# The last scan group of a Mamba-2 layer joins the common chunk order, and two products of the output projection take its place as filler

## The chip, the cores and the metric

The kernel runs on one core of one Trainium2 chip. The metric is the time of one execution on the device in microseconds (us). A core has five engines that run side by side, each with a queue of its own that it works through in order: TensorE (PE in the profile; its weight loads are PEld), VectorE (DVE), ScalarE (ACT), GpSimd (POOL) and SyncE (SP), which here does nothing but issue DMAs. ScalarE and GpSimd issue DMAs too. All transfers of the core share 16 DMA engines. An instruction waits on semaphores for what it reads and for the buffer that it writes, and everything behind it on its engine waits with it.

## The reference, cut to what matters

The program is two layers on 1024 tokens of width 1024 in float32, each with a residual: layer A is a chunked spatial gating MLP, layer B a Mamba-2 mixer, and a final RMSNorm follows. The change is in layer B:

```python
proj = h @ w_in                                   # 1024 x 6176: z | x | B | C | dt
xbc = silu(causal_depthwise_conv(xbc, conv_w, conv_b))        # 4 taps
# 8 groups g of 256 channels (4 heads), 8 chunks c of 128 tokens
cb = einsum('bclgn,bcsgn->bclsg', Cm, Bm)
w_ls = cb[..., None] * decay * dt[:, :, None]
y_diag = einsum('bclsgj,bcsgjp->bclgjp', w_ls, x)
states = einsum('bclgn,bclgj,bclgjp->bcgjpn', Bm, decay_to_end * dt, x)
# the state is carried from chunk to chunk: carry * dec + st
y_off = einsum('bclgn,bcgjpn,bclgj->bclgjp', Cm, prev, exp(dA_cs))
y = y_diag + y_off + x * d_skip
gated = rmsnorm_by_group(y * silu(z), norm_w)     # 8 groups of 256 channels
out = gated @ w_out                               # 2048 -> 1024, plus residual, then the final norm
```

## The kernel before, in words

**Products.** A float32 product is made of three products of rounded halves: an operand is split into a high part (a cast, by ScalarE, L111) and a low part (operand minus high part, by VectorE, L112), and `mm3` issues high·high, low·high and high·low (L134 to L136). "A step" below is six such matmuls of 128x128 by 512 columns. Large products are done as Strassen-Winograd schemes of seven products on half matrices (`Block` for the input projections, `Out` for the output projections); their sums of operand blocks are made on the way, for the input projection by VectorE and GpSimd (L204, L205 and neighbours), for the output projection by DMAs that add into SBUF (`add`, L682; `b12_plus`, L648 and L653; tiles ya and wb), which GpSimd issues.

**Layer B, input side.** `z_block(b)` makes the gate silu(z) of two groups as one Strassen block, and stores it to DRAM in `z_d`. Blocks 0 to 2 are 256 columns wide per half; block 3 is 128 wide, and makes the gate of group 6 alone. `Scan`'s other inputs x, B, C come from `xbc_block` for some groups, and for groups 2, 4, 6 and 7 from plain products by the generator `pj` (128 steps in all, tile ab). `convolve` puts the four convolution taps behind them on VectorE (L1182, and L1185 for the halo, tiles xc and bc).

**The scan.** `scans()` (written out by hand in `tc.manual_schedule()`) runs 56 chunks, groups 0 to 6 with 8 chunks each, in one pipeline. In chunk n it issues: `pe_b(n)` (four products on TensorE: L1427, L1431, L1437); steps of `pj` up to a target; `pe_a(n+2)` (transposes and C·B, L1395, L1396, tile tp); `update` and `out` (VectorE and GpSimd); `weights(n+1)` (L1419: the masked decay weights wl, which `pe_b(n+1)` needs); `decay(n+2)` (ScalarE, L1401, L1403; reads the tile wl that `load` fetched from cs_d, L1390); `tokens(n+2)` (L1409, L1411); `gate(n)` (L1470, GpSimd, by the gate tile ze); the queue of convolution taps, cleared by `drain`; `load(n+3)`. Half groups end with their sum of squares, a store of the gated result to DRAM (`g_d`, L1477), and, a group later, the inverse RMS (`rs_d`). `prefetch` brings a group's gate (L1359) and the decay broadcasts (L1362) into ze. The 128 steps of `pj` are spread over these 56 chunks, 16 ahead and 2 in each chunk, and so TensorE has 12 `mm3` matmuls beside the chunk's own 19 small ones.

**Group 7.** It comes behind `scans()`, and the tile scheduler orders it. `z_last` makes its gate as a plain product (96 matmuls of 512 columns) straight into SBUF (`Z`), so that group 7 needs neither `z_d` nor `g_d`. `last_steps` runs its 8 chunks with VectorE in the places where the other groups use GpSimd. `interleave` mixes these with `bo_first`: products 1 and 7 of the output projection `bo`, 32 steps, 192 matmuls (tile bo).

**The output projection.** `bo` is an `Out` with A = the gated result (tokens by 2048 channels) and B = the weight b_w_out. `fetch(n, c)` loads what product n needs of channel group c: A pieces ya (`load_a`, through `gscale`, which first loads the inverse RMS broadcast to 128 partitions, tile rb, L1649; then the piece, L1657; and then multiplies by norm weight and inverse RMS on VectorE, L1660) and B pieces wb (L642, 1 MB each). `prep(n, c)` splits both operands into xh, xl and wh, wl, and issues the sums by DMA. Products 2, 6, 4, 5 and 3 follow in `into_end`, where the residual is added (L792), the final norm is made and the result is stored.

Of the kernel before, what the change touches and what calls it, by code (L numbers as in the profile page):

```python
# [29 lines left out]
def kernel(  # L30
# [567 lines left out]
    class Out:  # L598
# [12 lines left out]
        def __init__(self, src, w, scale, res, accs, keep, ran):  # L611
# [3 lines left out]
            self.Y3 = []  # L615
# [9 lines left out]
        def load_a(self, i, kh, c):  # L625
# [30 lines left out]
        def prep(self, n, c):  # L656

            if (n, c) in self.ops:
# [4 lines left out]
                              6: ((0, 0), (0, 0)), 4: ((1, 1), (1, 0)), 5: ((1, 0), (0, 1))}[n]  # L663
            x, y = A(i, j, c), B(k, l, c)
# [5 lines left out]
            if n == 1:  # L670
                self.add(x, self.src[c][:, :, 512:1024] if self.scale is None else A(1, 0, c))
# [208 lines left out]
    def z_block(b, eng=nc.vector):  # L880

        wide = 256 if b < 3 else 128

        def done(name, i, a, u):
# [6 lines left out]
            g, m = (2 * b + j, i) if b < 3 else (6, j)  # L891
            nc.gpsimd.dma_start(out=z_d[g][:, m, th * 512:(th + 1) * 512], in_=zt)

        def W(kh, j):
            c = 512 * b + j * wide
            return [b_w_in[kh * 512:(kh + 1) * 512, c:c + wide]]

        return Block(H2, W, False, done, eng, wide)
# [32 lines left out]
    SPILT, AHEAD, LEFT = (0, 1, 3, 5), 16, 4  # L931
# [399 lines left out]
    def z_last(Z):  # L1331

        c = (G - 1) * 256
        W = [load_w([b_w_in[kh * 512:(kh + 1) * 512, c:c + 256]], 4) for kh in range(2)]
        for th in range(2):
            az = acc2("az")
            for kh in range(2):
                for m in range(2):
                    for k in range(4):
                        mm3(az[:, m, :], [w[:, k, m * P:(m + 1) * P] for w in W[kh]],  # L1340
                            [h_[:, k, :] for h_ in H2[f"A{2 - th}{kh + 1}"]], kh == 0 and k == 0, kh == 1 and k == 3)
                    if (kh, m) == (1, 1):
                        nc.scalar.activation(Z[:, :, th * 512:(th + 1) * 512], az, AF.Silu)
                    yield

# [5 lines left out]
    def prefetch(g, th):  # L1351
# [6 lines left out]
        if g < G - 1:  # L1358
            nc.sync.dma_start(out=ze[:, 0:2], in_=z_d[g][:, :, th * 512:(th + 1) * 512])  # L1359
# [6 lines left out]
    class Scan:  # L1366


        def __init__(self, g, eng):
            self.g, self.st, self.eng = g, sts[g], eng  # L1370
            self.wl, self.tp, self.cw, self.ps, self.state = {}, {}, {}, {}, {}
            if g < G - 1:
                gd.append(dr.tile([P, 2, T], F32, name=f"g_d{g}"))
            else:
                gd.append(self.st["Z"])
# [6 lines left out]
        def z(self, c, n=1):  # L1382
            if self.g == G - 1:
                return self.st["Z"][:, :, c * P:(c + n) * P]
            return self.st["ze", c // 4][:, 0:2, c % 4 * P:(c % 4 + n) * P]
# [87 lines left out]
        def squares(self, th):  # L1473
            sq = self.sq = q4([P, 2, 512], "gsq")
            nc.scalar.activation(sq, self.z(4 * th, 4), AF.Square)
            if self.g < G - 1:
                nc.sync.dma_start(out=gd[self.g][:, :, th * 512:(th + 1) * 512], in_=self.z(4 * th, 4))  # L1477
# [4 lines left out]
        def sum_b(self):  # L1482
            pr = sm("pr")
            n = 1 if self.g < G - 1 else 2
# [34 lines left out]
    def last_steps():  # L1519

        sc = Scan(G - 1, V)

        def a(c):
            sc.load(c), sc.pe_a(c), sc.decay(c), sc.tokens(c), sc.weights(c)

        a(0)
        yield
        for c in range(8):
            if c < 7:
                a(c + 1)  # L1530
                yield
            sc.pe_b(c), sc.carry(c), sc.update(c), sc.out(c)
            last = sc.gate(c)
            if c == 1:
                prefetch(G - 1, 1)
                rs = group_rstd(G - 2, 0, T)
            if c in (2, 3):
                rs[c - 2](last)
# [8 lines left out]
    def scans():  # L1547
# [33 lines left out]
        for n, (g, c) in enumerate(chunks):  # L1581
# [35 lines left out]
            if c == 4:  # L1617
                prefetch(g + 1, 0)
# [175 lines left out]
```

## Time and profile before

| | us |
|---|---|
| median of 3 runs | 1633.78 |
| lowest, highest run | 1629.82, 1635.27 |
| the profiled execution, own time | 1631.56 |
| its span in the trace | 1629.8 |
| chunk 53 of `scans()` to the end of products 1 and 7 (1377.14 to 1498.48) | 121.34 |
| products 2, 6, 4, 5, 3 with the end (1498.48 on) | 131.3 |

At 1377.14 the first matmul of chunk 53 of `scans()` (group 6, sixth chunk) starts. The span is the time from the first to the last recorded instruction. Busy times of engines are sums over the span; the share of a window has to be read for that window. The granted clock (PEclk) is the share of TensorE's full speed. A timeline row has the start in the span, the duration, engine, line, operation, tiles, and in brackets the idle time of the engine before it with the instruction or DMA that ended it. In the rows of the prediction "q1" is the DMA queue that SyncE feeds, and "q0" the one that GpSimd feeds.

### The profile page before, as it was taken

To read this page: it belongs to the slowest core of one execution; us is meant where nothing else is said; L and a number is where in the kernel's file an instruction comes from. 1 tells how busy PE (TensorE), PEld (TensorE's weight loads), DVE (VectorE), ACT (ScalarE), POOL (GpSimd) and SP (SyncE) were. 2 spreads that over 40 slices of the span, in tenths; PEclk is the share of its full clock that TensorE was granted. 3 is DMA by queue.
4 is the path that set the end of the run, shared out by engine and by line. 5 is a ranking of instruction groups with operands and counts; after the bars stand their busy time and mean duration, and the time that the engine had idled before them with its cause. 6 is when DMAs were issued, how large, how long until landed. Compare 5 with 4: busy or idle time off the path is not lost. (4 is left out here: it accounts for less than half of the span.)

```text
span 1629.8 us, 21273 instructions
## 1 busy us (share of the span) xinstructions
PE 1511.3 (93%) x7832; PEld 1245.5 (76%) x7832; DVE 1082.9 (66%) x1669; ACT 757.1 (46%) x1239; POOL 468.3 (29%) x477
## 2 busy tenths in 40 slices
PE   5799999999999897997899999999999999979988
PEld 5799988888888786775678777777777777757766
DVE  6966566666666543667744788587767767658656
ACT  4523233332324254544544454456667567544444
POOL 3601100000000231134203222407766756321231
PEclk8899999999999999998999999999999999989999
DMA  5154323333335999631253222447666575796993
GB/s 170 48 186 142 104 85 109 108 109 104 102 107 185 292 279 253 133 107 52 92 101 118 87 98 78 151 159 194 182 181 180 159 197 134 217 252 185 226 239 108
DMA packets 164872, 244.89 MB, mean 150 GB/s; under 512 B 16048, under 2 KB 96800, under 8 KB 161568
## 3 DMA queue, kind: packets, MB, share of 16 engines
q1 hardware_dynamic: 134672, 166.43, 34.6%
q0 software_dynamic: 20928, 63.45, 16.9%
q10 hardware_dynamic: 9168, 13.64, 2.3%
q8 instruction: 62, 1.02, 0.3%
q14 instruction: 42, 0.34, 0.1%
HBM read 169.23 MB, written 51.18 MB: 135 GB/s over the span
## 5 line engine op out<-in xcount | busy, mean ns | idle before, releaser
L134 PE MATMUL acc<-hh,wh 128*128 128x512 f32 x868 | 345.5, 398 | 14.5 <-ACT wh L111 4.0
L136 PE MATMUL acc<-hh,wl 128*128 128x512 f32 x868 | 343.4, 396 | 4.3 <-DVE wl L112 3.5
L135 PE MATMUL acc<-hl,wh 128*128 128x512 f32 x868 | 342.9, 395 | 4.4 <-DVE hl L964 4.4
L112 DVE TENSOR_TENSOR wl<-wr,wh 128x1024 fp32r<-128x1024 f32 x94 | 122.8, 1309 | 127.8 <-ACT wh L111 127.7
L134 PEld LDWEIGHTS acc<-hh,wh 128*128 128x128 f32 x868 | 166.2, 191 | 52.1 <-DVE u L1217 5.2
L136 PEld LDWEIGHTS acc<-hh,wl 128*128 128x128 f32 x868 | 165.8, 191 | 42.1 <-DVE wl L112 5.7
L135 PEld LDWEIGHTS acc<-hl,wh 128*128 128x128 f32 x868 | 166.1, 191 | 38.8 <-DVE hl L964 4.8
L111 ACT CAST wh<-wr 128x1024 fp32r<-128x1024 f32 (+1 forms) x113 | 116.2, 1030 | 113.7 <-PE acc L135 79.2
L252 ACT COPY u<-acc 128x512 f32<-128x512 f32 x117 | 68.0, 582 | 183.9 <-PE acc L136 182.6
L136 PE MATMUL acc<-wh,hl 128*128 128x256 f32 x448 | 130.8, 292 | 11.6 <-DVE hl L355 11.6
L134 PE MATMUL acc<-wh,hh 128*128 128x256 f32 x448 | 131.5, 293 | 4.1 <-DVE vt L291 2.5
L135 PE MATMUL acc<-wl,hh 128*128 128x256 f32 x448 | 130.1, 290 | 1.3 <-DVE wl L365 1.3
L1401 ACT ACTIVATE wl<-wl,tk 128x128 f32<-128x128 f32 x256 | 82.1, 392 | 86.3 <-DMA wl<-cs_d 85.9
L134 PE MATMUL ab<-hh,wh 128*128 128x512 f32 x256 | 116.5, 455 | 1.8 <-DVE u L1217 1.8
L112 DVE TENSOR_TENSOR xl<-ya,xh 128x1024 fp32r<-128x1024 f32 x40 | 48.9, 1223 | 80.1 <-ACT xh L111 79.9
L136 PE MATMUL ab<-hh,wl 128*128 128x512 f32 x256 | 101.3, 396 | 0.0
L135 PE MATMUL ab<-hl,wh 128*128 128x512 f32 x256 | 100.7, 393 | 0.0
L136 PEld LDWEIGHTS acc<-wh,hl 128*128 128x128 f32 x448 | 89.3, 199 | 12.5 <-DVE hl L355 12.5
L134 PEld LDWEIGHTS acc<-wh,hh 128*128 128x128 f32 x448 | 89.3, 199 | 5.1 <-issue 2.9
L134 PE MATMUL bo<-wh,xh 128*128 128x512 f32 x192 | 79.5, 414 | 14.4 <-ACT wh L111 6.0
L135 PEld LDWEIGHTS acc<-wl,hh 128*128 128x128 f32 x448 | 89.4, 200 | 1.7 <-DVE wl L365 1.5
L595 POOL DMA_DIRECT2D y_d<-y x8 | 4.4, 548 | 297.0 <-DVE y L592 297.0
(316 smaller groups left out, 3366.8 us busy)
## 6 DMA issues: line engine op xcount, KB each, us to landing
wr<-in_a_w_in_dram SPq DMA_DIRECT2D x48, 512.0 KB, 3.6
wl<-cs_d SPq DMA_DIRECT2D x64, 256.0 KB, 3.4
wr<-in_b_w_in_dram SPq DMA_DIRECT2D x30, 512.0 KB, 4.2
ya<-ya POOLq DMA_DIRECT2D x28, 512.0 KB, 15.8
wb<-in_a_w_out_dram SPq DMA_DIRECT2D x10, 1024.0 KB, 11.1
wb<-in_b_w_out_dram SPq DMA_DIRECT2D x10, 1024.0 KB, 18.7
wr<-in_b_w_in_dram SPq DMA_DIRECT2D x36, 256.0 KB, 3.8
v<-v_d SPq DMA_DIRECT2D x8, 1024.0 KB, 4.7
```

The costliest lines, as they stand in the source:

```text
L111: nc.scalar.copy(out=hi, in_=src)
L112: return (eng or nc.vector).tensor_tensor(out=lo, in0=src, in1=hi.bitcast(F32), op=ALU.subtract)
L134: nc.tensor.matmul(out=o, lhsT=l[0], rhs=r[0], start=start, stop=False, **kw)
L135: nc.tensor.matmul(out=o, lhsT=l[0], rhs=r[1], start=False, stop=False, **kw)
L136: nc.tensor.matmul(out=o, lhsT=l[1], rhs=r[0], start=False, stop=stop, **kw)
L252: nc.scalar.copy(out=self.u[n][:, i], in_=a)
L595: nc.gpsimd.dma_start(out=yd, in_=y)
L1401: nc.scalar.activation(wl[:, j, :], wl[:, j, :], AF.Relu, scale=-1.0, bias=tokc(2, c, self.g)[:, j:j + 1])
```

## The change

- `z_block(3)` is 256 columns wide like the others, and makes the gates of groups 6 and 7 in one Strassen block of 168 matmuls in place of 84. `z_last`, `last_steps`, `interleave` and `Z` are gone, and with them the 96 matmuls of the plain gate product.
- `scans()` runs all 64 chunks, group 7 like the others: GpSimd in its places, the gate through `z_d`, the gated result through `g_d`.
- `pj` is spread over the first 53 chunks (`LAST`). From chunk 54 on 26 (`FIRST`) of the 32 steps of `bo_first` fill the chunks, in the hand-written order; the other 6 run at the start of `into_end`.
- In `Out`, the scaling of a loaded A piece is no longer issued with the load: `load_a` keeps it as a closure, and `ready` runs it ahead of the `prep` or the sum that reads the piece. In `weights`, groups 6 and 7 each have an rb load of their own, as before.
- The first loads of `bo` are written at two places of `fill`: ahead of the last four steps of `pj`, if the target reaches `total - 4` in that call, and else with `bo.prep(1, 0)`, ahead of the last one. The targets are 16 + 112·(n + f)/53 for f = 1/2 and 1. They are 122.7 and 123.8 in chunk 50, after which 124 steps have been issued, and the first condition, `ran[0] < 124 <= upto`, holds in neither chunk 50 nor 51.

```diff
+            self.Y3, self.raw = [], {}
...
-                self.scale(raw, src, g, i)
+                self.raw[i, kh, c] = self.scale(raw, src, g, i)
+
+        def ready(self, *at):
+
+            if at in self.raw:
+                self.raw.pop(at)()
...
+            self.ready(i, j, c)
             x, y = A(i, j, c), B(k, l, c)
...
             if n == 1:
+                self.ready(1, 0, c)
                 self.add(x, self.src[c][:, :, 512:1024] if self.scale is None else A(1, 0, c))
...
             if n == 2:
+                self.ready(1, 1, c)
                 self.add(A(0, 0, c), A(1, 1, c))
...
-        wide = 256 if b < 3 else 128
...
-    SPILT, AHEAD, LEFT = (0, 1, 3, 5), 16, 4
+    SPILT, AHEAD, LEFT, LAST, FIRST = (0, 1, 3, 5), 16, 4, 53, 26
...
+    def bo_first():
+        yield from bo.product(1, lambda n, c: bo.fetch(1, min(c + 2, 3)))
+        for n, _ in enumerate(bo.product(7)):
+            if n in (4, 8, 12):
+                bo.fetch(2, n // 4 - 1)
             yield
...
-        chunks = [(g, c) for g in range(G - 1) for c in range(8)]
+        chunks = [(g, c) for g in range(G) for c in range(8)]
...
+        def fill(n, f):
+            upto = min(total, AHEAD + (total - AHEAD) * (n + f) / LAST)
+            if ran[0] < total - 4 <= upto:
+                project(total - 4)
+                for c in range(2):
+                    bo.fetch(1, c)
+            if ran[0] < total <= upto:
+                project(total)
+                bo.prep(1, 0)
+            project(upto)
+            if ran[0] == total:
+                drain(2)
+            while ran[1] < FIRST * (n + f - LAST - 1) / (N - LAST - 1):
+                next(first)
+                ran[1] += 1
...
-            project(want(.5))
+            fill(n, .5)
...
-            project(want(1))
-        project(total)
-        sc = scan[G - 2]
-        drain(len(queue))
-        sc.squares(1), sc.sum_a(), sc.sum_b(), sc.sum_c(1)
+            fill(n, 1)
+        sc = scan[G - 1]
+        sc.squares(1), sc.sum_b(2), sc.sum_c(1)
+        return first
...
-    for _ in range(NZ):
-        next(zl)
-    for c in range(2):
-        bo.fetch(11, c)
-    for _ in range(8 - NZ):
-        next(last_ssd)
-        next(zl)
-    for _ in zl:
-        pass
-    interleave(last_ssd, 9 + NZ, bo_first(), 32)
```

The orders below show three places. First VectorE, around the first scalings of the output projection. Before, they stand behind the convolution taps of bc, and behind `tokens` of group 7's first chunk (cw):

```order
L1182 SCALAR_TENSOR_TENSOR bc<-ab,par,bc 128x1023
L1182 SCALAR_TENSOR_TENSOR bc<-ab,par,bc 128x1022
L112 TENSOR_TENSOR wl<-wb,wh 128x1024
L1182 SCALAR_TENSOR_TENSOR bc<-ab,par,bc 128x1021
L1409 TENSOR_TENSOR cw<-tp,tk 128x256
L1411 TENSOR_TENSOR cw<-tp,mask 128x128
L1660 SCALAR_TENSOR_TENSOR ya<-ya,par,rb 128x512 x8
```

The same place of the changed kernel, on VectorE in chunk 53, from the first scaling to `weights(54)` (the last row); the two rows ya are the pieces of channel group 0:

```order
L1522 SCALAR_TENSOR_TENSOR ya<-ya,par,rb 128x512 x2
L112 TENSOR_TENSOR xl<-ya,xh 128x1024
L112 TENSOR_TENSOR wl<-wb,wh 128x1024
L1522 SCALAR_TENSOR_TENSOR ya<-ya,par,rb 128x512 x2
L1188 SCALAR_TENSOR_TENSOR bc<-ab,par,bc 128x1023
L1188 SCALAR_TENSOR_TENSOR bc<-ab,par,bc 128x1022
L1188 SCALAR_TENSOR_TENSOR bc<-ab,par,bc 128x1021
L1439 TENSOR_TENSOR state<-sp,state 128x256
L1445 TENSOR_TENSOR t_11414<-yy,ze 128x256
L1448 SCALAR_TENSOR_TENSOR cw<-x,dsk,yy 128x128 x2
L1404 TENSOR_TENSOR wl<-wl,cw 128x512
```

The scalings, the splits of `prep(1, 0)` and three taps now stand ahead of the state update, the output and the weights of a running scan.

Second SyncE, at the end of group 6, before: the loads of ya stand among those of the scan (wl), one or two at a time:

```order
L1477 DMA g_d_10832<-ze 256x1x512
L1502 DMA sv<-ss_d 128x8
L1362 DMA ze<-ecs_d 64x4x128 x4
L1390 DMA wl<-cs_d 128x512
L1657 DMA ya<-g_d_8218 128x2x512
L1657 DMA ya<-g_d_8619 128x2x512
L1390 DMA wl<-cs_d 128x512
```

The same place of the changed kernel, from the store of group 6's first half on:

```order
L1461 DMA g_d_10980<-ze 256x1x512
L1486 DMA sv<-ss_d 128x8
L1349 DMA ze<-z_d_5305 128x2x512
L1352 DMA ze<-ecs_d 64x4x128 x4
L1511 DMA rb<-rs_d 128x2x512
L1518 DMA ya<-g_d_8323 128x2x512
L647 DMA wb<-in_b_w_out_dram 128x4x512 x2
L1511 DMA rb<-rs_d 128x2x512
L1518 DMA ya<-g_d_8323 128x2x512
L1375 DMA wl<-cs_d 128x512
```

Six loads of the output projection, together 4 MiB, now stand in one row, behind the five loads of group 7's ze.

Third VectorE in the early output products, where the second half of group 7 is scaled (the last row of ya in each order). Before, the row ya<-Z stands behind the first split of product 6 (xl of L110) and ahead of product 2's additions to the result (u) and of the second split of product 6:

```order
L110 SCALAR_TENSOR_TENSOR xl<-ya,xh 128x1024
L112 TENSOR_TENSOR wl<-wb,wh 128x1024
L1660 SCALAR_TENSOR_TENSOR ya<-Z,par,rb 128x512 x2
L792 TENSOR_TENSOR u<-bo,u 128x512
L813 TENSOR_SCALAR stats<-stats 128x1
L792 TENSOR_TENSOR u<-bo,u 128x512
```

In the changed kernel, the same scaling, now of a piece ya from DRAM, behind the second split of product 6 and most of those additions:

```order
L110 SCALAR_TENSOR_TENSOR xl<-ya,xh 128x1024
L112 TENSOR_TENSOR wl<-wb,wh 128x1024
L821 TENSOR_SCALAR stats<-stats 128x1
L800 TENSOR_TENSOR u<-bo,u 128x512
L821 TENSOR_SCALAR stats<-stats 128x1
L1522 SCALAR_TENSOR_TENSOR ya<-ya,par,rb 128x512 x2
```

The scaling moved behind one more split and four additions. What it waits for (rb, by way of rs_d) is the same.

More of the change, by code (lines that the diff above doesn't have):

```diff
@@ L1517, in group_rstd @@
         return guess, tail
[L1519 to L1538, printed above, removed]
-            if c % 4 == 3:
-                sc.squares(c // 4), sc.sum_b(), sc.sum_c(c // 4)
-            if c == 3:
-                half = group_rstd(G - 1, 0, 512)
-            if c in (4, 5):
-                half[c - 4](last)
+    rbs = {}
@@ new lines, with accs_b @@
+    outr = out.rearrange("(c p) d -> c p d", p=P)
+    def accs_b(n):
+        if n == 1:
+            return [t[:, i, :] for t in [acc2("bo") for _ in range(2)] for i in range(2)]
+        return [sm("bo") for _ in range(4)]
+    bo = Out(gd, b_w_out, gscale, lambda t, nb: h1_d[t][:, nb * 512:(nb + 1) * 512], accs_b, False, (1, 7, 2))
+    def bo_first():
[3 more added lines that the diff above has]
+                bo.fetch(2, n // 4 - 1)
@@ L1740, in hook @@
                     bo.prep_unit(0)
+        for _ in first:
+            pass
         bo.ran = Out.ORDER
```

118 lines of the change are left out of this document (38 added, 80 removed).

## The prediction

> **What bounds the kernel now.** The page first:
>
> ```profile
> span 1629.8 us, 21273 instructions
> PE 1511.3 (93%) x7832; PEld 1245.5 (76%) x7832; DVE 1082.9 (66%) x1669; ACT 757.1 (46%) x1239; POOL 468.3 (29%) x477
> ```
>
> TensorE is busy for 93% of the span: a change pays by fewer matmuls or by fewer stretches in which TensorE waits or runs at half clock. So I read windows next, each set to a stage that the change touches (columns: window, length, busy time and instructions of PE, PEld, DVE, ACT, POOL, then granted clock, DMA share, GB/s).
>
> ```profile
> core 0: us, PE busy (x) PEld busy (x) DVE busy (x) ACT busy (x) POOL busy (x), PEclk, DMA share, GB/s
> 985.00:1010.00 25.00, 25.00 (x112) 20.68 (x112) 18.81 (x24) 10.67 (x19) 8.38 (x6) 1.00 0.29 87
> 1010.20:1036.00 25.80, 19.50 (x73) 14.10 (x72) 18.45 (x25) 13.21 (x21) 10.93 (x9) 0.93 0.39 123
> 1377.14:1498.48 121.34, 106.46 (x541) 80.81 (x541) 80.62 (x154) 63.58 (x103) 32.46 (x33) 0.94 0.78 211
> ```
>
> The first is a wide Strassen block at its best: 112 matmuls in 25.00 us, 0.223 us each. The second is the narrow block of group 6's gate: 73 matmuls take 25.80 us, 9.5 above 73 x 0.223 = 16.3. The third runs from chunk 53 of the scan to the end of products 1 and 7. What a chunk needs of itself comes from the TensorE timeline, where two chunks start:
>
> ```profile
> 1372.16 0.66 PE L1427 MATMUL yy<-wl,cw 128*64 128x128 f32 x8
> 1377.14 0.66 PE L1427 MATMUL yy<-wl,cw 128*64 128x128 f32 x8
> ```
>
> They lie 4.98 us apart with 12 filler matmuls between, so a chunk's own work is 4.98 - 12 x 0.223 = 2.30 us. The third window holds 11 chunks (25.3 us) and 36 last matmuls of pj, 96 of z_last and 192 of products 1 and 7 (324 x 0.223 = 72.3): 97.6 of 121.34 us. The other **23.7 us are lost** in waits and slow matmuls, such as these (in brackets the wait before):
>
> ```profile
> 1427.57 0.80 PE L134 MATMUL bo<-wh,xh 128*128 128x512 f32 x1 [3.88 <-ACT Z L1343]
> 1446.73 0.80 PE L136 MATMUL bo<-wh,xl 128*128 128x512 f32 x1 [4.20 <-DVE xl L112]
> 1447.32 0.63 PE L134 MATMUL bo<-wh,xh 128*128 128x512 f32 x1
> 1447.74 0.63 PE L135 MATMUL bo<-wl,xh 128*128 128x512 f32 x1
> ```
>
> After a wait, matmuls start 0.42 us apart (1447.32, 1447.74), not 0.223: a long wait costs about 2 us more than its idle time, with some ten slow matmuls at 0.2.
>
> **The change part by part.**
>
> *Matmuls.* 84 more in the block, 96 fewer without z_last: -12 x 0.223 = **-2.7 us**.
>
> *The wide block.* The narrow one lost 9.5 us. Wide neighbours lose less, by the waits at their joints:
>
> ```profile
> 922.43 0.80 PE L134 MATMUL acc<-hh,wh 128*128 128x512 f32 x1 [2.88 <-DVE u L1217]
> 1076.23 0.47 PE L134 MATMUL ab<-hh,wh 128*128 128x512 f32 x1 [1.85 <-DVE u L1217]
> ```
>
> A block twice as long has twice the TensorE time to hide its sums. I take a loss of 3.5, above these joints because block 3 comes last: **-6.0** (a loss of 2, or the full 9.5 and more if the sums bind, which is a rival).
>
> *The old last stretch.* Its 23.7 us go with the separate order: **-23.7**. What is late next is the changed order itself.
>
> *First new wait, chunk 54.* By the code, the first loads of `bo` are issued with `prep(1, 0)` at the end of chunk 52, and VectorE's first scaling, behind which `weights(54)` stands, waits for the last of them. SyncE issues them behind a store and five loads for ze. Z is the start of chunk 53.
>
> ```profile
> 1354.90 0.61 SPq L1359 DMA_DIRECT2D ze<-z_d  x1
> 1374.73 3.04 SPq L1362 DMA_DIRECT2D ze<-ecs_d  x4
> 1392.00:1396.00 4.00, 4.00 (x20) 3.30 (x19) 0.92 (x1) 3.11 (x6) 0.00 (x0) 1.00 1.03 367
> 1396.00:1400.00 4.00, 4.00 (x19) 3.33 (x18) 3.96 (x4) 2.34 (x3) 0.00 (x0) 1.00 1.03 351
> ```
>
> Chunk 52's issues end at 1374.73 + 3.04 = 1377.77; with one more load of ze (z_d, 0.61, which group 7 did not have) the burst starts at Z + 1.2. Its 4.19 MB at the mean of 367 and 351 GB/s take 11.7, and 1.5 from issue to first bytes is my choice: landed at Z + 14.4.
>
> ```profile
> 1406.17 5.76 DVE L1660 SCALAR_TENSOR_TENSOR ya<-ya,par,rb 128x512 f32<-128x512 f32 x8
> 1395.09 2.60 DVE L1182 SCALAR_TENSOR_TENSOR bc<-ab,par,bc 128x1023 f32<-128x1023 f32 x2 [3.41 <-ACT bc L1188]
> 1378.98 0.42 DVE L1454 TENSOR_TENSOR state<-sp,state 128x256 f32<-128x256 f32 x1 [1.29 <-PE sp L1437]
> 1380.85 0.42 DVE L1409 TENSOR_TENSOR cw<-tp,tk 128x256 f32<-128x256 f32 x1
> ```
>
> VectorE then does two scalings of 5.76 / 8 = 0.72 (Z + 15.8), three taps of 1.30 (Z + 19.7), and state to weights as between 1378.98 and 1380.85, 1.9: weights(54) at Z + 21.6. TensorE has 2.3 of its own in chunk 53 and no filler. It waits 19.3, with 2 slow after it: **+21.3** (16, if the ya piece lands well ahead of the whole burst; 26, at the 263 GB/s of a row below).
>
> *Second new wait, chunk 57.* For channel group 2 another six loads, 4 MiB, wait for a buffer that chunk 53's gate on GpSimd frees; behind them stand the decay loads wl of chunks 57 and 58, and behind the splits and scalings of `prep(1, 2)` stands `weights(57)`.
>
> ```profile
> 1375.33 1.12 POOL L1466 TENSOR_TENSOR cw<-cw,t 128x256 f32<-128x256 f32 x1 [1.91 <-DVE cw L1463]
> 1377.56 0.72 POOL L1470 TENSOR_TENSOR ze<-ze,cw 128x256 f32<-128x256 f32 x1
> 1380.30 1.26 ACT L1401 ACTIVATE wl<-wl,tk 128x128 f32<-128x128 f32 x4
> 1382.00 1.05 ACT L111 CAST wh<-wr 128x1024 fp32r<-128x1024 f32 x1 [0.44 <-PE ab L135]
> 1382.95 0.62 ACT L1403 ACTIVATE wl<-wl 128x512 f32<-128x512 f32 x1
> 1397.60 1.22 DVE L112 TENSOR_TENSOR wl<-wb,wh 128x1024 fp32r<-128x1024 f32 x1
> ya<-g_d SPq DMA_DIRECT2D x11, 512.0 KB, 5.9
> ```
>
> GpSimd needs 1375.33 to 1378.28, 3 us, from out to the end of the gate: issued about Z + 24. 11.7 of loading, 1.5 to the first bytes and some 2.7 of an accumulating 0.5 MB beside it (half the 5.9 of a 512 KB load) land it at Z + 40; then wl, the decays (1.26 + 0.62), a split's cast (1.05), two splits of 1.2, two scalings of 0.72 and 1.6 for tokens and weights end at Z + 49. TensorE arrives with chunks 54 to 56 and 6 steps done at about Z + 42: **+6.9** (0 to 12).
>
> *Two small ones.* weights(58) behind `prep(1, 3)`, and `prep(7, 0)` behind the accumulate of `b12_plus(1, 0)`: **+4.7** together (0 to 10), about the size of the 4.20 and 3.88 waits above.
>
> *The tail.* These waits of product 2 come as the scaling of group 7's second half waits for its rb:
>
> ```profile
> 1521.09 1.42 DVE L1660 SCALAR_TENSOR_TENSOR ya<-Z,par,rb 128x512 f32<-128x512 f32 x2 [3.04 <-DMA rb<-rs_d]
> 1527.36 0.50 PE L134 MATMUL bo<-wh,xh 128*128 128x512 f32 x1 [1.69 <-ACT wh L111]
> 1528.82 0.50 PE L135 MATMUL bo<-wl,xh 128*128 128x512 f32 x1 [0.95 <-DVE wl L112]
> q0 software_dynamic: 5088, 13.63, 71.7%
> ```
>
> The scaling now stands behind one more split, so 1.69 + 0.95 = 2.6 can go. About 1 MB of group 7's pieces is added between 1500 and 1600, where the accumulating queue alone takes 71.7% of the DMA engines. I take **-1.5** (-4.6, with slow matmuls, to +5, two loads of 512 KB at the rate above where nothing hides them). The round trip of group 7 through DRAM is hidden elsewhere: its gate is loaded half a group ahead.
>
> *Sum:* -2.7 - 6.0 - 23.7 + 21.3 + 6.9 + 4.7 - 1.5 = **-1.0 us**, against the profiled execution's 1631.56 us (span 1629.8): 1630.6. The median of the runs is 2.2 above that execution: **1633 us**. About 0.3%, 4.9 us, is what a measurement of this kernel can tell from no change.
>
> **The rivals.**
>
> *Faster: one wait only.* The waits overlap. What is late by 21 us on VectorE in chunk 53 lets every load behind it catch up, and the second burst has then as long to land as TensorE takes. For it: the burst is issued by SyncE, not by VectorE. Against it: wl(57) stands behind it in the queue. The second wait and the small ones fall from 11.6 to 3: -1.0 - 8.6 = -9.6, **1624 us**.
>
> *Slower: the second burst is starved.* It shares the DMA engines with the accumulating DMAs of `prep(1, 0)` and `prep(1, 1)`.
>
> ```profile
> 1432.00:1436.00 4.00, 4.00 (x19) 3.31 (x18) 1.03 (x4) 1.94 (x2) 0.00 (x0) 1.00 1.12 263
> ```
>
> Here the engines are full and move 263 GB/s, not 359. 4.19 MB then take 15.9, 4.2 more: the second wait is 11.1. The small ones, which hang on such DMAs, go to their 8, and the tail, which is fullest, to +3: -1.0 + 4.2 + 3.3 + 4.5 = +11.0, **1645 us**. It decides if the burst runs under 300 GB/s. The Trainium skill, "DMA: Bandwidth & Descriptors", section "Queues, rings and completion order", states that each DMA engine takes its queue rows in turn, a packet at a time. By that rule a load of SyncE's queue keeps only part of the engine while GpSimd's queue has work, which speaks for this rival; no row here separates it from fuller memory traffic.
>
> *Slower: the wide block stays bound.* GpSimd's sums and VectorE's taps get in each other's way.
>
> ```profile
> 1005.91 1.75 POOL L205 TENSOR_TENSOR t<-wr,t 128x512 f32<-128x512 f32 x1
> 1036.95 2.39 POOL L205 TENSOR_TENSOR t<-wr,t 128x1024 f32<-128x1024 f32 x1 [2.73 <-DMA wr<-in_b_w_in_dram]
> L1185 DVE SCALAR_TENSOR_TENSOR xc<-halo,par,xc x6: 206/1237/1246, 1004.6 to 1019.3; 128x1 f32<-128x1 f32 x2, 128x2 f32<-128x2 f32 x2, 128x3 f32<-128x3 f32 x2
> L1185 DVE SCALAR_TENSOR_TENSOR xc<-halo,par,xc x6: 207/208/2350, 940.9 to 959.2; 128x1 f32<-128x1 f32 x2, 128x2 f32<-128x2 f32 x2, 128x3 f32<-128x3 f32 x2
> ```
>
> The tiny halo taps have a median of 1237 ns from 1004 to 1019, where GpSimd sums, and of 208 ns from 941 to 959. The wide sums take 2.39 instead of 1.75. If the block keeps its 9.5, the sum rises by 6 to +5; if it loses 5 more, to +10: **1639 to 1644**. It decides if the block's sums take longer than its 168 x 0.223 = 37.5 us. The Trainium skill, "SBUF — State Buffer", section "SBUF: two separate sides", says that GpSimd and a VectorE operation with two SBUF inputs share a port pair that one of them holds for a whole instruction. By that rule these halo taps wait out a GpSimd sum, as their medians show.
>
> *The early loads do fire.* Then the first burst starts two chunks, 2 x 4.98 = 10 us, earlier, and the first wait is so much shorter: **1623**. By the targets, 122.7, 123.8 and 124.8 around 124 steps, they don't.
>
> **How the numbers follow.** The forecast gets 0.42. One wait only 0.30, the early loads 0.02, the starved burst 0.16, the wide block 0.10. Within the forecast, ten parts in 42 fall outside 4.9 us, five on each side. Faster is 0.30 + 0.02 + 0.05 = 0.37, same 0.32, slower 0.16 + 0.10 + 0.05 = 0.31. The forecast alone is 1633 with 1625 to 1641. The range 1618 to 1648 adds the faster case with its first wait at 16 (-5, about 1618) and the starved burst with a tail at +5 (about 1648).
>
> **What would show it.** Right: one TensorE wait of 14 to 24 us ahead of L1412 (`pe_b`) in chunk 54, ended by wl of L1404, and a VectorE scaling that waits for ya or wb just before; a second of up to 12 three chunks later; bursts at 350 to 370 GB/s; the wide block in about 41 us (37.5 + 3.5); 0.223 us per filler matmul between. Wrong: the loads of `bo` ahead of chunk 52; no wait in chunk 57; waits of several us in each group-7 chunk, which would mean that bo's splits, and not loads, set the pace; a block of 47 us or more.

## The result and the profile after

The changed kernel takes 1685.01 us (median of 4 runs, 1683.02 to 1686.52) where the kernel before takes 1634.53 (4 runs): a ratio of 1.0309, with an interval of 1.0287 to 1.0330. It is 3.1% slower; the forecast was no change, and the range ended at 1648. The profiled execution took 1684.17 us, with a span of 1682.5. By stage, from the two traces (starts of the same instructions; the forecast as the prediction's terms fall on the stages):

| stage | before | after | difference | forecast |
|---|---|---|---|---|
| to the first matmul of the scan (contains block 3) | 1099.61 | 1125.90 | +26.3 | +12.7 (84 matmuls, 18.7, less 6.0) |
| chunks 0 to 52 | 277.53 | 294.85 | +17.3 | +8.0, the 36 matmuls moved here |
| chunk 53 to the end of products 1 and 7 | 121.17 | 116.07 | -5.1 | -20.2 (-21.4 - 8.0 - 23.7 + 32.9) |
| products 2, 6, 4, 5, 3 and the end | 131.49 | 145.68 | +14.2 | -1.5 |
| sum | 1629.8 | 1682.5 | +52.7 | -1.0 |

Every stage came out worse than forecast, by 9 to 16 us each. Of the 26.3 in the first row 2.6 lie ahead of anything that was changed: the joint between two blocks ahead of block 3, a row of the prediction, stands at 922.43 before and at 924.99 after. The windows of block 3, chunks 0 to 52, the stretch from chunk 53 on, and the tail of the changed kernel:

```profile
core 0: us, PE busy (x) PEld busy (x) DVE busy (x) ACT busy (x) POOL busy (x), PEclk, DMA share, GB/s
1010.00:1054.00 44.00, 34.20 (x141) 27.32 (x140) 26.06 (x29) 16.69 (x24) 27.00 (x14) 0.88 0.29 92
1125.90:1420.75 294.85, 279.23 (x1688) 212.50 (x1688) 190.94 (x427) 187.13 (x398) 190.54 (x217) 0.99 0.62 161
1420.75:1536.82 116.07, 78.09 (x404) 59.15 (x404) 68.72 (x125) 54.67 (x93) 46.09 (x54) 0.81 0.82 228
1536.82:1682.50 145.68, 119.51 (x481) 94.79 (x479) 83.76 (x128) 63.59 (x91) 33.07 (x36) 0.90 0.80 194
```

In the third row TensorE is busy for 78.09 of 116.07 us, and its clock was granted to 0.81; in the same stretch before it was 106.46 of 121.34 at 0.94. Less work takes nearly the same time. The waits of TensorE that matter, from the timeline of the changed kernel (in brackets the wait ahead):

```profile
1031.36 0.80 PE L134 MATMUL acc<-hh,wh 128*128 128x512 f32 x1 [8.60 <-ACT wh L111]
...
1294.28 0.66 PE L1412 MATMUL yy<-wl,cw 128*64 128x128 f32 x8 [2.79 <-ACT wl L1386]
...
1447.05 1.12 PE L1412 MATMUL yy<-wl,cw 128*64 128x128 f32 x8 [24.02 <-issue]
...
1475.81 1.12 PE L1412 MATMUL yy<-wl,cw 128*64 128x128 f32 x8 [8.18 <-DVE wl L1404]
...
1528.45 1.86 PE L1471 MATMUL pr<-gsq,ones 128*1 128x256 f32 x8 [3.92 <-ACT gsq L1460]
...
1570.80 0.80 PE L135 MATMUL bo<-wl,xh 128*128 128x512 f32 x1 [3.15 <-DVE stats L821]
...
1620.83 0.79 PE L134 MATMUL bo<-wh,xh 128*128 128x512 f32 x1 [8.21 <-ACT wh L111]
```

In this order: one in block 3, one of the smaller ones in the scan, the two that the prediction named (chunks 54 and 57), a new one before the last sums of squares, and two in the tail. Each was followed back.

**Block 3.** ScalarE casts wh at 1030.26, late because it waited for a convolution tap. VectorE and GpSimd in that time:

```profile
1008.00 2.95 DVE L1188 SCALAR_TENSOR_TENSOR xc<-u,par,xc 128x511 f32<-128x511 f32 x1
1010.87 2.35 DVE L1191 SCALAR_TENSOR_TENSOR xc<-halo,par,xc 128x1 f32<-128x1 f32 x1
1013.14 0.74 DVE L1188 SCALAR_TENSOR_TENSOR xc<-u,par,xc 128x510 f32<-128x510 f32 x1
1013.81 2.35 DVE L1191 SCALAR_TENSOR_TENSOR xc<-halo,par,xc 128x2 f32<-128x2 f32 x1
1016.07 2.95 DVE L1188 SCALAR_TENSOR_TENSOR xc<-u,par,xc 128x509 f32<-128x509 f32 x1
```

```profile
1008.00 2.39 POOL L112 TENSOR_TENSOR wl<-wr,wh 128x1024 fp32r<-128x1024 f32 x1 [4.68 <-ACT wh L111]
1010.35 2.85 POOL L204 TENSOR_TENSOR t<-wr 128x1024 f32<-128x1024 f32 x1
1013.28 2.85 POOL L205 TENSOR_TENSOR t<-wr,t 128x1024 f32<-128x1024 f32 x1
1016.09 2.39 POOL L214 TENSOR_TENSOR wr<-wr 128x1024 f32<-128x1024 f32 x1
```

```profile
1021.33 0.63 ACT L1217 ACTIVATE xc<-xc 128x512 f32<-128x512 f32 x1 [12.06 <-DVE xc L1191]
```

The operations of VectorE and GpSimd end in turns. A halo tap of one column, which takes 0.21 us elsewhere (at 1000.20), takes 2.35 beside a GpSimd sum. ScalarE waits 12.06 us for the taps' end, and the cast that TensorE needs stands behind it.

**The scan.** ScalarE at chunk 28, with 12 filler matmuls and 10.34 us long:

```profile
1283.72 1.91 ACT L1289 ACTIVATE bc<-bc 128x2048 f32<-128x2048 f32 x1
1285.54 1.19 ACT L1194 ACTIVATE x<-ab,par 128x1024 f32<-128x1024 f32 x1
1286.63 0.72 ACT L1475 COPY srow<-pr 1x256 f32<-1x256 f32 x2
```

A SiLU over a whole bc, the first tap of the next product and the copy of a sum of squares follow one another there, all ahead of the decays (L1386). The SiLUs over a whole x or bc start in chunks 4, 12, 20, 28, 36 and 44 before the change, always at the same place of a group, and in chunks 3, 12, 19, 27 (this one, 0.2 us ahead of 28), 34 and 42 of the changed kernel.

**Chunks 54 and 57.** The issues of the first burst by SyncE, and the two scalings that wait for its pieces:

```profile
1422.08 1.73 SPq L1511 DMA_DIRECT2D rb<-rs_d  x1
...
1427.33 2.59 SPq L1518 DMA_DIRECT2D ya<-g_d  x1
```

```profile
1431.80 1.41 DVE L1522 SCALAR_TENSOR_TENSOR ya<-ya,par,rb 128x512 f32<-128x512 f32 x2 [11.70 <-DMA ya<-g_d]
...
1439.93 1.42 DVE L1522 SCALAR_TENSOR_TENSOR ya<-ya,par,rb 128x512 f32<-128x512 f32 x2 [3.19 <-DMA ya<-g_d]
...
1446.27 0.68 DVE L1404 TENSOR_TENSOR wl<-wl,cw 128x512 f32<-128x512 f32 x1
```

The burst starts 1.3 us after chunk 53 (1420.75), as forecast (1.2), and its last piece is there at 1439.93, 19.2 us after chunk 53 and not 14.4. From its first issue to that landing (1422.08 to 1439.93) the DMA engines moved 316 GB/s in the mean, 5.6 MB: the burst of 4.19 MB did not have them to itself, as the five loads for ze are issued just ahead of it and two more pieces ya of 512 KB at 1431.16. From the landing to the matmul of 1447.05 it is 7.1 us, where the prediction had 7.2. The row of that matmul names no releaser; the wl of L1404 that it reads ends at 1446.95. For chunk 57 the row is one of ScalarE, whose decay waits for a load behind the second burst:

```profile
1467.37 1.28 ACT L1386 ACTIVATE wl<-wl,tk 128x128 f32<-128x128 f32 x4 [9.56 <-DMA wl<-cs_d]
```

**The tail.** VectorE, with the moved scaling (L1522) behind two additions (L800) that wait for the residual's load, and GpSimd, whose row of nine sums by DMA starts behind that scaling:

```profile
1567.79 0.69 DVE L800 TENSOR_TENSOR u<-bo,u 128x512 f32<-128x512 f32 x1 [2.39 <-DMA u<-h_d]
...
1573.33 0.69 DVE L800 TENSOR_TENSOR u<-bo,u 128x512 f32<-128x512 f32 x1 [2.52 <-DMA u<-h_d]
...
1574.95 1.42 DVE L1522 SCALAR_TENSOR_TENSOR ya<-ya,par,rb 128x512 f32<-128x512 f32 x2
```

```profile
1562.82 0.86 POOL L689 DMA_DIRECT2D ya<-ya  x1 [4.53 <-issue]
...
1576.89 0.86 POOL L689 DMA_DIRECT2D ya<-ya  x1 [12.32 <-ACT wh L111]
```

The profile names a ScalarE cast as the releaser; by the code the DMA waits for the scaling, which ends at 1576.37. In the kernel before, the same row started 24.7 us after product 2:

```profile
1523.03 0.87 POOL L682 DMA_DIRECT2D ya<-ya  x1 [6.41 <-issue]
```

Now it is 1576.89 - 1536.82 = 40.1 us.

### The profile page after: what moved, and what is told of

The parts are those of the page before. It is cut to its first block, busy times and chain, and to the rows that moved or that the text cites. A ratio compares the mean times of both kernels' runs of the same rounds, so it can differ in the third digit from the quotient of the medians.

```text
span 1682.5 us, 21265 instructions
## 1 busy us (share of the span) xinstructions
PE 1520.7 (90%) x7816; PEld 1253.1 (74%) x7816; DVE 1069.8 (64%) x1649; ACT 758.1 (45%) x1240; POOL 495.2 (29%) x502
## 3 DMA queue, kind: packets, MB, share of 16 engines
q1 hardware_dynamic: 135392, 169.59, 33.8%
## 5 line engine op out<-in xcount | busy, mean ns | idle before, releaser
L134 PE MATMUL acc<-hh,wh 128*128 128x512 f32 x896 | 356.3, 398 | 16.5 <-ACT wh L111 9.9
L136 PE MATMUL acc<-hh,wl 128*128 128x512 f32 x896 | 354.8, 396 | 5.7 <-DVE wl L112 4.5
L135 PE MATMUL acc<-hl,wh 128*128 128x512 f32 x896 | 354.5, 396 | 4.4 <-DVE hl L970 4.4
L134 PEld LDWEIGHTS acc<-hh,wh 128*128 128x128 f32 x896 | 171.8, 192 | 54.4 <-ACT wh L111 10.7
L112 DVE TENSOR_TENSOR wl<-wr,wh 128x1024 fp32r<-128x1024 f32 x92 | 119.2, 1298 | 140.3 <-ACT wh L111 140.3
L136 PEld LDWEIGHTS acc<-hh,wl 128*128 128x128 f32 x896 | 171.5, 191 | 44.6 <-DVE wl L112 6.6
L135 PEld LDWEIGHTS acc<-hl,wh 128*128 128x128 f32 x896 | 171.5, 191 | 40.1 <-DVE hl L970 4.9
L111 ACT CAST wh<-wr 128x1024 fp32r<-128x1024 f32 x111 | 116.2, 1050 | 116.5 <-PE acc L135 84.4
L1386 ACT ACTIVATE wl<-wl,tk 128x128 f32<-128x128 f32 x256 | 81.7, 392 | 86.4 <-DMA wl<-cs_d 86.2
L134 PE MATMUL bo<-wh,xh 128*128 128x512 f32 x192 | 83.3, 434 | 11.8 <-ACT wh L111 11.8
## 6 DMA issues: line engine op xcount, KB each, us to landing
ya<-ya POOLq DMA_DIRECT2D x28, 512.0 KB, 12.4
wb<-in_a_w_out_dram SPq DMA_DIRECT2D x10, 1024.0 KB, 23.7
```

Of the source, the lines that this page charges most:

```text
L111: nc.scalar.copy(out=hi, in_=src)
L112: return (eng or nc.vector).tensor_tensor(out=lo, in0=src, in1=hi.bitcast(F32), op=ALU.subtract)
L134: nc.tensor.matmul(out=o, lhsT=l[0], rhs=r[0], start=start, stop=False, **kw)
L135: nc.tensor.matmul(out=o, lhsT=l[0], rhs=r[1], start=False, stop=False, **kw)
L136: nc.tensor.matmul(out=o, lhsT=l[1], rhs=r[0], start=False, stop=stop, **kw)
L1386: nc.scalar.activation(wl[:, j, :], wl[:, j, :], AF.Relu, scale=-1.0, bias=tokc(2, c, self.g)[:, j:j + 1])
```

## The experiments

Gains are told by the ratios to the kernel before (each set of runs has its own), times its median of about 1631 us.

### e1: the scaling of the tail moved back

```diff
                 bo.fetch(22, 3)
                 bo.sums(2, 2)
+                bo.ready(1, 1, 3)
```

> The changed kernel with one row moved on VectorE: the scaling of group 7's second half, `ready(1, 1, 3)`, is issued right after `sums(2, 2)`, ahead of product 2's additions and of the second split of product 6, where the kernel before had it. In the changed kernel GpSimd's row of nine sums by DMA starts at 1576.89, 40.1 us after the start of product 2 (1536.82); before it was 24.7 (1523.03 after 1498.31). Theory 1 (the late scaling holds up the sums, and these hold up products 4 and 5): the row of sums starts 12 to 15 us earlier, the 8.21 us wait at the start of product 5 falls below 3 us, and the time falls by 10 to 14 us, to 1671 to 1675. Theory 2 (group 7's extra megabyte in full DMA queues is what makes the tail long): the sums start earlier, but land as late as now, and the time stays within 5 us of 1685. My prediction, which saw a gain in the later scaling: 2.6 us slower than now, 1688.

Measured: 1671.62 us, ratio 1.0245 (1.0218 to 1.0272), 10.4 us less than the changed kernel. The tail takes 136.47 us instead of 145.68. GpSimd's row of sums, and the wait at the start of product 5, in e1:

```profile
1562.86 1.32 POOL L689 DMA_DIRECT2D ya<-ya  x1
```

```profile
1612.53 0.50 PE L134 MATMUL bo<-wh,xh 128*128 128x512 f32 x1 [2.75 <-ACT wh L111]
```

The row starts 27.7 us after product 2 (1535.13), 12.4 us earlier, and the 8.21 us wait is 2.75. Theory 1 holds; for the extra megabyte there is no more than the 5.0 us by which this tail is still longer than before's 131.49. My reading of this move as a gain had the wrong sign.

### e2: the early loads made to fire

```diff
-            if ran[0] < total - 4 <= upto:
+            if ran[0] <= total - 4 <= upto:
```

> The changed kernel with `<` made `<=` in the condition of the early loads, so that they are issued in the first half of chunk 51, about 1.5 chunks or 7.5 us ahead of the end of chunk 52. Theory 1 (the first wait, 24.0 us idle ahead of chunk 54, is the time that the burst takes to land): it falls by 7 to 10 us, to 14 to 17, and the time by 7 to 10, to 1675 to 1678. Theory 2 (VectorE's work between the landing and the weights of chunk 54, the scalings, splits, taps and the state, sets it): the wait stays above 20 us and the time within 5 us of 1685.

Measured: 1672.59 us, ratio 1.0256 (1.0233 to 1.0279), 8.6 us less. TensorE and ScalarE at the first wait of e2:

```profile
1433.16 1.12 PE L1412 MATMUL yy<-wl,cw 128*64 128x128 f32 x8 [16.53 <-DVE wl L1404]
```

```profile
1419.75 1.28 ACT L1386 ACTIVATE wl<-wl,tk 128x128 f32<-128x128 f32 x4 [10.69 <-DMA wl<-cs_d]
```

The wait falls from 24.0 to 16.5, and the stretch from chunk 53 on by 8.0 us (108.12). Theory 1 holds, but now the burst hits something else: the decays of a chunk wait 10.69 us for their wl of 256 KB, issued behind it in SyncE's queue.

### e3: block 3's sums on VectorE

```diff
-            zb[3].eng = nc.gpsimd
-            zb[3].run(unit=convolve, lo=nc.gpsimd)
+            zb[3].run(unit=convolve)
```

> The changed kernel with the sums and the low parts of the wide block on VectorE in place of GpSimd; the convolution taps stay where they are. Theory 1 (VectorE's taps wait for GpSimd's sums, operation by operation): no halo tap in the block is longer than 0.3 us, the 8.60 us wait at 1031 falls below 4 us, and the scan starts 5 to 10 us earlier than 1125.90; the time is 1675 to 1680. Theory 2 (the block is bound by how much work the taps and sums are together): VectorE now has about 20 us more to do, TensorE waits as long or longer for it, and the scan starts at 1126 or later; the time is 1685 to 1695.

Measured: 1674.53 us, ratio 1.0266 (1.0251 to 1.0281), 7.0 us less. The halo taps of e3's block, and its wait:

```profile
L1191 DVE SCALAR_TENSOR_TENSOR xc<-halo,par,xc x10: 210/215/218, 995.4 to 1014.7; 128x3 f32<-128x3 f32 x4, 128x1 f32<-128x1 f32 x3, 128x2 f32<-128x2 f32 x3
```

```profile
1018.35 0.79 PE L134 MATMUL acc<-hh,wh 128*128 128x512 f32 x1 [3.63 <-ACT wh L111]
```

No tap is longer than 218 ns, and the wait is 3.63 instead of 8.60, although VectorE took over the sums. Theory 1 holds: the amount of VectorE's work grew and the wait fell. The edit changes two things at once, as each sum also takes less time on VectorE (the last section has the numbers); what ties the 8.60 us to the taps is ScalarE's 12.06 us wait for them. From the joint at 918.19 (922.43 before the change) to the scan it is now 195.8 us; in the changed kernel it is 200.9, before it was 177.2. So this part is 5.1 us; 18.6 us more than before remain, which is the 84 added matmuls (18.7) and nothing saved.

### e4: two filler steps a chunk

```diff
-            upto = min(total, AHEAD + (total - AHEAD) * (n + f) / LAST)
+            upto = min(total, AHEAD + 2 * (n + f) if n + f <= 47 else 110 + 3 * (n + f - 47))
```

> The changed kernel with the filler at two steps a chunk, as before the change, up to chunk 47, and three a chunk from there to chunk 53; the sum of the steps and where they end are the same. Theory 1 (the pace of 2.11 steps moves the ends of the plain products against the chunks, so that convolution taps and SiLUs stand ahead of decays and weights): chunks 0 to 46 lose about as little as before the change, waits of 0.5 us and more in chunks 0 to 52 fall from seven to four or fewer, and chunk 53 starts 5 to 9 us earlier after chunk 0 than the 294.85 us now. Theory 2 (the waits come from elsewhere, such as loads that are late): the 294.85 us stay within 2 us.

Measured: 1673.44 us, ratio 1.0261 (1.0243 to 1.0279), 7.8 us less. The window of chunks 0 to 52 in e4:

```profile
1125.56:1412.20 286.64, 279.67 (x1688) 213.62 (x1687) 200.47 (x427) 185.88 (x397) 191.30 (x218) 0.99 0.61 166
```

The same 1688 instructions of TensorE take 8.2 us less than in the changed kernel. 286.64 is before's 277.53 with the 36 moved matmuls (8.0) and 1.1. Only two waits of over 0.9 us are left in it, of 2.88 and 2.80 us, both ended by ScalarE's copy of a sum of squares (srow), like the two in the kernel before (2.58 and 2.88). The SiLUs are back in chunks 4, 12, 20, 28, 36 and 44. Theory 1 holds.

### e5: the four edits together

> The changed kernel with the four edits of e1 to e4 together: scaling early in the tail, first loads of the output projection ahead of prep(1, 0) (in the second half of chunk 51), block 3's sums and low parts on VectorE, filler at two steps a chunk up to chunk 47. If the four losses are separate, as theory 1 of each has it, the gains add up: 13.4 + 12.4 + 10.5 + 11.6 = 47.9 us by the medians, 1637, and 5 us more or less as these medians carry. If they hide one another (a queue that is late anyway, one DMA backlog behind all four), the gain is under 38 us and the time over 1647.

Measured: 1645.86 us, ratio 1.0091 (1.0065 to 1.0116): 35.6 us less than the changed kernel. By the ratios the four gains add up to 10.4 + 8.6 + 7.0 + 7.8 = 33.8, and the stages say the same: the four edits alone took 9.2, 8.0, 5.1 and 8.2 us from theirs, 30.5, and e5 takes 34.4 from the four together (195.2 from the joint to the scan, 289.4, 103.4, 135.1). So the losses are separate, as far as intervals of some 4 us a run can tell. The result lies between the two outcomes as they were written. The 47.9 of the expectation took medians of different sets of runs, and these carry some us that are not the edits': the joint ahead of block 3 alone, where nothing was changed, lies between 918.1 and 925.2 in the traces shown here.

### e6 and e7: the first loads and prep(1, 0) still earlier

Both put the loads of `bo.fetch(1, 0)` and `bo.fetch(1, 1)` in the first half of chunk 50, and the sums of squares behind three of the six left steps; e7 also puts `bo.prep(1, 0)` at the end of chunk 51.

```diff
+        EN, EP = 50, 99
...
+            if (n, f) == (EN, .5):
+                for c in range(2):
+                    bo.fetch(1, c)
...
-        sc.squares(1), sc.sum_b(2), sc.sum_c(1)
+        sc.squares(1)
+        for _ in range(3):
+            next(first)
+        sc.sum_b(2), sc.sum_c(1)
```

> As e5, with the first loads still earlier (first half of chunk 50), and with the partial sums of group 7's second half (L1471) behind three of the six left steps of products 1 and 7, so that these cover the 3.8 us wait for ScalarE's squares. If what is left of the first wait (16.5 us in e2) is the load of chunk 54's decay inputs standing behind the burst in the DMA queue, it falls below 11 us; if it is VectorE's work, taps and splits ahead of weights(54), about 9 us of it, it stays there at 11 to 16. The wait ahead of L1471 falls below 1 us either way. Time 4 to 10 us below e5.

> As e6, with prep(1, 0) at the end of chunk 51 in place of 52. If VectorE's work ahead of weights(54) is what is left of the first wait, it falls by the two scalings and splits, 5 us, against e6; if the landing of the loads is what is left, the wait only moves one chunk forward (chunk 53), as long as before, and the time is within 3 us of e6.

Measured: e6 1650.37 us, ratio 1.0119 (1.0092 to 1.0145); e7 1648.28, ratio 1.0102 (1.0069 to 1.0135). Neither differs from e5 or from the other beyond the intervals. The waits of e7 at chunks 53 and 54:

```profile
1410.72 1.12 PE L1411 MATMUL yy<-wl,cw 128*64 128x128 f32 x8 [9.92 <-DVE wl L1403]
1419.40 1.12 PE L1411 MATMUL yy<-wl,cw 128*64 128x128 f32 x8 [4.49 <-issue]
```

In e6 they are 3.90 and 9.79 us: the same 14 us, the larger part one chunk later. So taking VectorE's work out of the way did not shorten what is left; ScalarE waits 12.08 us for a wl in e7, as it waits 10.69 in e2. The sums of squares wait no longer, but the tail grows by about as much (140.1 us in e6 and 139.9 in e7, 135.1 in e5). The load of rb for group 7's second half is issued 20.1 and 20.5 us after the start of product 2 there, and 13.5 in e5; that this is what makes the tail longer was not tested. Expected gains of 4 to 10 us did not come.

### e8: the wide block alone, in the kernel before

```diff
-        wide = 256 if b < 3 else 128
+        wide = 256
...
-            g, m = (2 * b + j, i) if b < 3 else (6, j)
+            g, m = 2 * b + j, i
...
-        W = [load_w([b_w_in[kh * 512:(kh + 1) * 512, c:c + 256]], 4) for kh in range(2)]
-        for th in range(2):
-            az = acc2("az")
...
+        nc.sync.dma_start(out=Z, in_=z_d[G - 1])
+        for _ in range(8):
+            yield
```

> The kernel before with the wide block alone: block 3 makes the gates of groups 6 and 7, and group 7's gate is loaded into Z from z_d in place of the plain product; scan order, filler and tail as before the change. By the prediction the block takes 12.7 us more and the 96 matmuls of z_last go (21.4 us): 5 to 9 us faster than before, if nothing else waits. By theory 1 of e3 (VectorE's taps wait for GpSimd's sums) the scan starts 22 to 27 us later than before's 1099.6, and the time is within 6 us of before. A third outcome: z_last also hid the first loads of the output projection, so that waits of 10 us and more appear ahead of its products; then it is slower than before by 5 to 15 us.

Measured: 1662.41 us, ratio 1.0210 (1.0184 to 1.0237), 34 us slower than before. The third outcome, and far larger than I gave it. The profiled execution, the shortest of the four, is 26.7 us longer than the profile before. Joint to scan takes 201.0 us, as in the changed kernel, so the block costs the same 23.8 us here. And the stretch from chunk 53 to the end of products 1 and 7, with 96 matmuls (21.4 us) fewer than before, takes 126.24 us where it took 121.17. TensorE and VectorE in it, and ahead of them the row of the kernel before that matches the first:

```profile
1404.30 0.60 PE L1487 MATMUL pr<-gsq,ones 128*1 128x256 f32 x4 [1.39 <-POOL gsq L1480]
```

```profile
1426.82 1.02 PE L1478 MATMUL pr<-gsq,ones 128*1 128x256 f32 x4 [13.48 <-POOL gsq L1471]
...
1437.82 0.79 PE L134 MATMUL bo<-wh,xh 128*128 128x512 f32 x1 [7.66 <-ACT xh L111]
```

```profile
1435.28 5.39 DVE L1651 SCALAR_TENSOR_TENSOR ya<-ya,par,rb 128x512 f32<-128x512 f32 x8 [14.08 <-DMA rb<-rs_d]
```

The sum of squares starts 27.7 us after chunk 53 in e8 (1426.82 - 1399.13) and 27.2 before (1404.30 - 1377.14): without z_last TensorE comes to it early and waits 13.48 us where it waited 1.39. In the kernel before z_last's matmuls lie from 1391.19 to 1419.63, across that time. ScalarE, which squares for it, had waited 5.37 us for a load of wb and 4.10 for convolution taps. Then VectorE waits 14.08 us for rb, a load of the output projection. Work of 11 x 2.30 + 228 x 0.223 = 76.1 us stands in 126.2: 50 us are lost, near the 47.9 (116.07 less 25.3 and 192 x 0.223) that the changed order loses in the same stretch. Both orders lack the 96 matmuls of z_last. That the loss has the same cause in both is not shown. Nor is e8 that one change alone: group 7 is ordered by the scheduler, and without z_last it orders the rest anew. The first load of rb is issued 23.1 us after chunk 53 (1422.22), where it was 17.3 before (1394.40).

### e9: VectorE's sums in the kernel before

The edit of e3 in the kernel before, whose block 3 is narrow.

> The kernel before, with one edit: the sums and low parts of its narrow block 3 on VectorE in place of GpSimd, as in e3. If the taps that wait for GpSimd's sums also make the narrow block's loss of 9.5 us, its halo taps fall from 1.24 to 0.2 us, the 2.77 us wait ahead of it goes, and the time falls by 3 to 6 us, to 1625 to 1628 beside a median of 1631: it would beat both kernels by a little. If the loss is the block's own shape (84 matmuls to hide the sums of a whole block), VectorE's added work costs as much as the taps save, and the time is within 3 us of before.

Measured (12 runs): 1629.93 us, ratio 0.9994 (0.9980 to 1.0007): no difference. The halo taps of e9:

```profile
L1185 DVE SCALAR_TENSOR_TENSOR xc<-halo,par,xc x14: 210/214/219, 984.9 to 1022.7; 128x2 f32<-128x2 f32 x5, 128x3 f32<-128x3 f32 x5, 128x1 f32<-128x1 f32 x4
```

The long taps are gone here too, and nothing is won: joint to scan takes 178.1 us, 177.2 before. The narrow block's 9.5 us have another cause, which stays open.

### e10: the first loads spread over three chunks

As e5, but without the two conditions of `fill`: the weight piece (0, 0) is loaded in chunk 50, (0, 1) in chunk 51, the pieces of A in chunk 52, and `bo.prep(1, 0)` runs at the end of chunk 53.

> As e5, but the first loads do not stand in one row: the two weight pieces of 1 MB are issued in chunks 50 and 51, the pieces of A with their rb in chunk 52, each behind the decay load wl of a chunk, and prep(1, 0) stands at the end of chunk 53, behind weights(54). In e2, e6 and e7 ScalarE waited 10 to 12 us for a wl that stood in the DMA queue behind the 4 MiB. If that is what the first wait is made of, no wait of over 4 us is left in chunks 51 to 54, and the time is 5 to 9 us below e5's 1646. If the DMA engines are simply full there (scan and output projection together), the same waiting shows up as several waits of 2 to 5 us in chunks 51 to 56, and the time is within 4 us of e5. In both cases it stays behind the kernel before, as the second burst, the block and the tail still cost what they do in e5.

Measured: 1641.41 us, ratio 1.0051 (1.0032 to 1.0070), about 6 us below e5 by the ratios, with intervals that just overlap. The first wait of e10:

```profile
1411.25 1.12 PE L1411 MATMUL yy<-wl,cw 128*64 128x128 f32 x8 [5.31 <-issue]
```

It was 10.07 in e5, and no wait of ScalarE for a wl is left around it. 5.31 is more than the 4 that I allowed; chunk 53 still has no filler, and two edits were made at once. Nor is the shorter wait a gain: chunks 53 and 54 together take 23.02 us (1403.65 to 1426.67) and took 21.89 in e5 (1406.69 to 1428.58), with the same matmuls, as the scalings and splits of `bo.prep(1, 0)` now hold up chunk 54 (waits of 1.06, 1.21 and 1.63 us). The wait ahead of chunk 57 fell from 9.90 to 5.15, and the stretch from chunk 53 on from 103.37 to 100.88. Another 4.3 us of the profiled execution lie in chunks 0 to 52 (285.12, and 289.42 in e5), and their cause stays open. Neither outcome came as it was written. It is the best version of the new order, and still slower than the kernel before.

## Why the prediction was wrong

- **Matmuls** (-2.7): right as a count. But TensorE's count was not what bound the stretch from which the 96 left (e8).
- **The wide block** (-6.0): wrong. "A block twice as long has twice the TensorE time to hide its sums" did not hold: 200.9 - 177.2 = 23.7 us more, against 18.7 of matmuls, so it loses 14.5 and not 3.5. The rival named the mechanism and the price (5 more than the narrow block's 9.5), with a chance of 0.10. e3 shows it: the 5 us go with GpSimd's sums. The rule of the Trainium skill that the prediction cited beside it ("SBUF — State Buffer", section "SBUF: two separate sides") fits these runs: taps of 2.35 us beside GpSimd's sums, 0.21 without them. The hoped-for saving of 6 is not there even then, and where the narrow block's 9.5 us come from stays open (e9). The sign of being wrong that I had written, a block of 47 us or more, came: 37.5 + 14.5 = 52.
- **Chunks 0 to 52** (no term): the step that was missing. I counted the 36 matmuls and took the pace of 2.11 steps for the same as 2. At 2, a product of 16 steps ends every 8 chunks, at the same place of a group; at 2.11 the ends drift, and their SiLUs and taps fall on sums of squares and decays. e4: 8.2 us.
- **The old last stretch** (-23.7): wrong in its cause. I gave the lost time to "the separate order". e8 keeps that order in the code and takes z_last out, and the loss grows to 50. So the order alone did not make the loss, and z_last's 21.4 us of matmuls covered waiting that is there without them: for VectorE's and ScalarE's work, and for loads of the output projection. How much of the 50 is the scheduler's new order stays open. I took both the matmuls (-21.4) and the lost time (-23.7) out, and in the sum all hung on what I put in their place, the next term.
- **The waits** (+32.9): the mechanism was right for both (burst, then scalings, taps and weights; wl behind the second burst), the sizes were low. Chunk 53 to 54 lost 24.0 + 3.7, not 21.3: the burst landed after 19.2 us, not 14.4, as I gave it the DMA engines to itself, and I priced TensorE's slow time after a wait at 2. Chunk 57 lost 8.2 and 3.8 after it, not 6.9; of the 3.8 a wait ahead of chunk 58 is 1.86, which I had among the small ones, and the rest are slow matmuls. The rest, with a wait of 3.92 before the sums of squares that I had not seen, is 47.9 - 39.7 = 8.2, not 4.7.
- **The tail** (-1.5): wrong in sign, +14.2. I asked which wait the scaling caused where it stood (2.6 us), and not who waits for it where it goes: behind additions that wait for the residual, ahead of GpSimd's nine sums. e1 gives 9.2 of it back. The other 5.0 are within the bound that I gave for the extra loads, and were not tested apart.
- **The early loads** do not fire, as I had read; e2 shows that it costs 8 us.
- **The starved burst** did not come as priced, but it was not far: windows of 4 us from 1451 to 1467, while the second burst lands, show 278 to 386 GB/s, 323 in the mean, between the 359 of the forecast and the rival's 263, with one of the four under its line of 300.

The misses add up: 2.6 ahead of the change, 11.0 for the block, 9.3 for the scan, 15.1 for the stretch from chunk 53, 15.7 for the tail, which is 53.7 of 52.7 + 1.0. The range was too narrow in a plain way: it let one rival come at a time, while the losses are separate (e5) and four of them came together; the pace, and a tail of +14.2, were in no rival.

## What to carry to other kernels

Before you book removed matmuls or an old wait as saved, ask what they covered: here 21 us of matmuls stood where other work and loads were waited for, and without them the stretch did not get shorter. When an operation moves on an in-order engine, price both ends: the wait it caused at the old place, and those who wait for it at the new one, DMA issues of other engines above all. And a change in pace is a change in alignment: filler of another step count per chunk moves the ends of products onto other work.

## What the runs showed of the hardware

The clock after the 24.02 us wait, in windows of 4 us of the changed kernel, the first two while TensorE is idle and the burst lands:

```profile
1429.00:1433.00 4.00, 0.00 (x0) 0.00 (x0) 1.20 (x2) 0.00 (x0) 0.00 (x0) 0.50 1.05 399
1433.00:1437.00 4.00, 0.00 (x0) 0.00 (x0) 2.63 (x3) 3.60 (x5) 0.00 (x0) 0.50 1.04 386
1447.00:1451.00 4.00, 3.95 (x17) 3.27 (x18) 2.89 (x5) 1.93 (x3) 3.98 (x4) 0.50 0.04 11
1451.00:1455.00 4.00, 4.00 (x18) 3.08 (x18) 4.00 (x6) 3.28 (x7) 0.00 (x0) 0.70 0.81 290
```

The granted clock is 0.50 in the idle time and stays there for the first 4 us of work, and the window after has 0.70: this wait of 24.02 us cost 3.7 us beyond its idle time, where I had taken 2 from a wait of 4.2. A sum of 128x1024 took 2.39 to 2.85 us on GpSimd beside taps, and 1.22 on VectorE (the rows L204 and L205 of e3's timeline).
